# Backward states of an mLSTM moved up among the last key sweeps, and seven chunks instead of four taken ahead of the attention stage

## The chip, the cores and the metric

The kernel runs on one core of a Trainium2 chip. The metric is the device time of one execution in microseconds (us); lower is better. Engines are named as in the profile: PE is TensorE (matmuls), PEld its weight loads, DVE VectorE, ACT ScalarE, POOL GpSimd, and SP the engine whose queue issues most of the DMAs. Every engine works through its own instructions in program order.

## The reference

One bidirectional encoder layer on 2048 tokens of 1024 channels. What matters here is the mLSTM group (4 heads of 128 channels), a scan in each direction, and what surrounds it:

```python
u = _rms_norm(h, norm_mix_g[l]);  proj = u @ w_in[l]
hy = _short_conv_centred(proj[..., :HY_COLS], ...)          # Hyena: long convolutions
y_hy = _group_rms_norm(_hyena(hy, spec, hy_skip[l]), ...)
qk = silu(_short_conv_centred(proj[..., HY_COLS:off], ...)) # queries and keys of the mLSTM
y_ml = _mlstm_bidirectional(q, k, v, o_pre, gates, ml_gate_b[l])
h = h + concatenate([y_hy, _group_rms_norm(y_ml, ...)]) @ w_out[l]
h = h + _cross_attention(_rms_norm(h, ...), _rms_norm(mem, ...), wq, wk, wv, wo)
h = h + square(relu(_rms_norm(h, ...) @ ff_w1[l])) @ ff_w2[l]
return _rms_norm(h, final_norm_g)

# one chunk of the mLSTM, per head; C, n, m are the carried state
s   = einsum('td,sd->ts', qc, kc) * w
num = s @ vc + inter * (qc @ C);   den = sum(s) + inter * (qc @ n)
h   = num / max(|den|, exp(-m_t))
C   = carry_decay * C + einsum('s,sd,se->de', we, kc, vc)
```

The backward direction is the same scan on the flipped sequence; both directions are added.

## The kernel before

The kernel writes the work of many generators; each `yield` is a point at which another may go on. The program's main function (`program`, from line 2100) combines them with a few helpers: `chain` one after the other, `weave` two in proportion to costs, `among(g, h, n)` one step of `h` behind each n-th step of `g` and the rest of `h` at the end, `beside_each(g, h)` a step of `h` behind every step of `g`. A scheduler then fixes the order on each engine: it goes by the written order and by its own estimate of when inputs are ready, so that work of one generator can stand among another's where buffers and data allow. PSUM is two sets of four banks, `mm` and `hy`, handed out in turn; who takes a bank waits until its user of four turns before has been read.

The stages around the change, in order of time:

- **Key sweeps and natural products** (`sweep`, `natural`, lines 748 to 897). The input projection is done for half the tokens at a time. Columns are swept transposed (q, k and the Hyena inputs), each product as three matmuls (`mm3`, L355, L358, L359) with its operands split into a high and a low part. Columns 8 and 9 are the keys. Values and the output gate are done in natural order by `natural`; tiles 0 and 1 are the values. The second half of the tokens (rows 1024 and up) is done first, the first half last. The **Hyena** convolution (`hyena`, L956, L987, L1030, L173 and L186 on PE) is woven in.
- **Gates** (`gates`, lines 1076 to 1174): six steps, which turn the gate columns into decays and weights (`cols`). They stand behind every second step of the sweep of columns 4, 5, 8, 9 of the first half.
- **Backward states** (`states` and `backward`, lines 1209 to 1225): 15 updates from chunk 15 down to chunk 1, a chunk being 128 tokens. An update loads keys `kn` and values `va` (L1178, L1184, two buffers of each), scales the values on POOL (L1196), makes four products on PE (L1200, `hy<-va,kn`), adds them to the decayed state on DVE (L1206) and stores it with a POOL DMA (L1219, `cbd`). In the kernel before they begin behind the products of the values of the first half, one step behind each step of values, columns 6 and 7, and tile 2; what is left of them follows at the end.
- **Memory's products** (`memproj`, from line 693): 128 products L708, 64 keys' products L725 and 32 values' products L737 in plain float32, in which one instruction is two records of the trace. Their weights come by `wm` loads (L415).
- **Chunks of the mLSTM** (`mlstm`, lines 1227 to 1364): for each of 16 chunks the scores (L1284, made one chunk ahead), their masked exponentials (POOL L1290 and L1291, ACT L1293, DVE L1275 and L1294), 16 products with values and states (L1322 `hy<-va,rw` and L1324 `hy<-cf,rw` or `hy<-cbn,rw`; the very first chunk has no forward state and so 12), the division on ACT and DVE (L1327 to L1338), and the update of the forward state (L1200 `hy<-ve,kn`, then DVE L1202 or L1206 into `cf`). Chunk 0 needs the last backward state, which is loaded as `cbn` (L1258). Behind each odd chunk two chunks are normalised together on DVE (`bank_rsqrt`, L211 to L216, then L1356).
- **Attention stage** (`attention`, from line 1438): it transposes the mixed rows (L1479), splits them into `act`, multiplies them by `w_out`, and goes on to the cross-attention. Its first four token groups need chunks 0 to 3 of the mLSTM.

In the kernel before, `take(m, 5)` takes the set-up of the chunks and chunks 0 to 3 behind the steps of the memory's products; chunks 4 to 15 are then woven with the attention stage.

Of the kernel before, what the change touches and what calls it, by code (L numbers as in the profile page):

```python
# [2076 lines left out]
def chain(*gens):  # L2077
    for g in gens:
        yield from g


def weave(a, b, wa, wb, until=False):
    da = db = 0.0
    fa = fb = False
    while not (fa and fb):
        if fb or (not fa and da / wa <= db / wb):
            try:
                da += next(a)
            except StopIteration:
                fa = True  # L2090
        else:
            try:
                db += next(b)
            except StopIteration:
                fb = True
                if until:
                    return


def program(p):  # L2100
    with ExitStack() as ms:
        with ExitStack() as es:
            p.inproj_open(es)
            p.filters_open()
            p.prepq = p.x_first()
            p.pop()
            s = chain(p.sweep(range(4), 0, True, lambda: p.prep_x(1)), p.opened(), p.sweep(range(4), 1, False))
            f = p.filters()
            for _ in range(5):
                next(s)  # L2110
            next(f)
            next(f)
            next(s)
            weave(s, f, 140, 102, True)
            p.gates_open(es)
            n = p.memproj()
            m = p.mlstm(ms)
            with ExitStack() as hs:
                rest = chain(s, p.sweep(range(4, 10), 1, True), p.natural(1, (3, 0, 1, 2), True),
                             p.natural(0, (3,)), among(p.sweep((4, 5, 8, 9), 0, False), p.gates(), 2),  # L2120
                             among(chain(p.natural(0, (0, 1)), p.sweep((6, 7), 0, False),
                                         p.natural(0, (2,), p.prep_mem, 2)), p.states(), 1),
                             )
                weave(rest, p.hyena(hs), 445, 329)
            for _ in chain(p.turned_in(), take(n, 1), beside_each(n, take(m, 5))):
                pass
        with ExitStack() as rs:
            p.ts = rs.enter_context(ExitStack())
            p.tail_open(p.ts)
            with ExitStack() as at:  # L2130
                g = p.attention(at)
                weave(g, m, 440, 112, True)
                ms.close()
                p.ffn_open(rs)
                for _ in g:
                    pass
            p.ffn()


def among(g, h, every):  # L2140
    for i, v in enumerate(g):
        yield v
        if i % every == every - 1:
            next(h, None)
    for _ in h:
        pass


def beside_each(g, h):
    for v in g:  # L2150
        yield v
        yield next(h, 0)
    yield from h


def take(g, n):
    for _ in range(n):
        v = next(g, None)
        if v is None:
            return  # L2160
        yield v
# [31 lines left out]
```

## Time and profile before

| | |
|---|---|
| three timed runs | 3066.46, 3072.43, 3081.08 us (median 3072.43) |
| profiled execution's own time | 3076.22 us |
| its span | 3074.5 us |
| mean granted TensorE clock | 0.987 |
| last backward update on PE | 1086.33 us |
| DVE, ACT, POOL busy in the span | 63%, 49%, 41% |
| HBM traffic over the span | 196 GB/s |

Times within the trace are us from the start of the span. A row of the timeline gives the start, the length, engine, line, operation, what is written from what, the shape, and how many records were merged; in square brackets stands how long the engine had been idle before it and what ended the wait. A row of the windows gives the length of a stretch, then busy time and records of each engine, the granted TensorE clock (1.00 is full speed), the DMA engines' busy share and GB/s. Lengths of single matmuls overlap; how long one really takes is the distance of two starts.

### The profile page before, as it was taken

Reading aid. Unit: us, or ns where it says so; the run is one execution under the profiler, and the core shown is the slowest. Engines: PE = TensorE matmul, PEld = TensorE weight load, DVE = VectorE, ACT = ScalarE, POOL = GpSimd, SP = SyncE. Lnnn points to the kernel's source line nnn. Section 1 sums busy time; section 2 is a strip of 40 time slices with the busy share of each in tenths; the row PEclk is TensorE's granted clock in tenths of the full one; section 3 lists DMA queues with packets and bytes.
Section 4 is the critical chain, followed back from the end, with each engine's and each line's share of the span. In section 5 each row is a group of like instructions: output and inputs, shape, how many; then the busy total and the mean of one; then the engine's idle time right before and its main releaser. Section 6 shows DMA issues by size and latency. Waiting matters only on the chain.

```text
span 3074.5 us, 44129 instructions
## 1 busy us (share of the span) xinstructions
PE 2984.5 (97%) x14799; PEld 2369.8 (77%) x14799; DVE 1938.8 (63%) x3442; ACT 1493.0 (49%) x2930; POOL 1259.7 (41%) x1025
## 2 busy tenths in 40 slices
PE   9999999998999988999999999999999999999998
PEld 7666667775678757888887888888888888888876
DVE  7855454657656347867665665557555676566695
ACT  6443455635654236555544455556555543333335
POOL 0112123411344654333133247765566374344653
PEclk9999999999999988999999999999999999999999
DMA  6655687596877965464567466657544565344434
GB/s 219 196 188 171 214 271 219 184 297 200 258 223 249 349 231 192 158 220 131 188 203 259 147 210 216 208 181 243 186 154 151 195 198 171 118 158 120 155 103 164
DMA packets 423643, 607.03 MB, mean 197 GB/s; under 512 B 36846, under 2 KB 229998, under 8 KB 422392
## 3 DMA queue, kind: packets, MB, share of 16 engines
q1 hardware_dynamic: 395972, 525.42, 53.3%
q0 software_dynamic: 18992, 62.96, 5.6%
q10 hardware_dynamic: 8452, 15.83, 1.4%
q8 instruction: 117, 1.92, 0.3%
q14 instruction: 110, 0.90, 0.1%
HBM read 401.67 MB, written 202.41 MB: 196 GB/s over the span
## 4 chain that ended last, share of the span: by engine, by line
PE 58%; DVE 2%; DMA 1%; issue 1%; ACT 0%; POOL 0%; SPq 0%; DVEq 0%; ACTq 0%; POOLq 0%
PE mm L355 12%; PE mm L359 12%; PE mm L358 12%; PE hy L355 6%; PE hy L359 6%; PE hy L358 6%; PE hy L1322 1%; PE hy L1324 1%; DVE bl L1693 0%; PE hy L1284 0%; PE hy L1479 0%; PE hy L1596 0%; DVE acc L1991 0%; PE hy L1200 0%; DVE acc L2028 0%
## 5 line engine op out<-in xcount | busy, mean ns | idle before, releaser
L1692 ACT CAST ah<-w 128x512 fp32r<-128x512 f32 x284 | 176.7, 623 | 304.0 <-PE hy L358 157.8
L1693 DVE TENSOR_TENSOR bl<-wr,bh 128x512 fp32r<-128x512 f32 x213 | 235.5, 1110 | 131.1 <-ACT bh L1692 131.0
L366 DVE TENSOR_TENSOR wl<-wn,wh 128x512 fp32r<-128x512 f32 (+1 forms) x296 | 216.6, 775 | 94.3 <-ACT wh L366 94.3
L355 PE MATMUL mm<-xh,wh 128*128 128x512 f32 x640 | 263.3, 413 | 3.7 <-ACT wh L366 1.2
L358 PE MATMUL mm<-xl,wh 128*128 128x512 f32 x640 | 254.1, 397 | 4.5 <-DVE xl L366 4.4
L1692 ACT CAST bh<-wr 128x512 fp32r<-128x512 f32 x232 | 143.4, 621 | 229.0 <-PE mm L359 177.5
L359 PE MATMUL mm<-xh,wl 128*128 128x512 f32 x640 | 253.7, 397 | 0.0
L1693 DVE TENSOR_TENSOR al<-w,ah 128x512 fp32r<-128x512 f32 x236 | 213.6, 905 | 55.7 <-ACT ah L1692 55.6
L359 PE MATMUL mm<-bh,al 128*128 128x512 f32 x576 | 223.7, 391 | 4.0 <-DVE al L1693 4.0
L355 PE MATMUL mm<-bh,ah 128*128 128x512 f32 x576 | 225.8, 392 | 0.1
L358 PE MATMUL mm<-bl,ah 128*128 128x512 f32 x576 | 224.9, 390 | 0.0
L366 ACT CAST wh<-wn 128x512 fp32r<-128x512 f32 (+1 forms) x296 | 164.4, 620 | 105.8 <-PE mm L359 51.0
L358 PE MATMUL mm<-act,wh 128*128 128x512 f32 x512 | 202.0, 394 | 0.0
L355 PE MATMUL mm<-act,wh 128*128 128x512 f32 x512 | 199.4, 396 | 2.0 <-ACT wh L366 1.9
L359 PE MATMUL mm<-act,wl 128*128 128x512 f32 x512 | 199.9, 392 | 0.0
L355 PE MATMUL hy<-bh,ah 128*128 128x512 f32 x448 | 175.2, 391 | 0.0
L358 PE MATMUL hy<-bl,ah 128*128 128x512 f32 x448 | 174.6, 390 | 0.0
L359 PE MATMUL hy<-bh,al 128*128 128x512 f32 x448 | 174.4, 390 | 0.0
L331 POOL TENSOR_TENSOR b<-b 128x512 f32<-128x512 f32 x32 | 48.1, 1505 | 294.6 <-DVE b L330 275.2
L355 PEld LDWEIGHTS mm<-xh,wh 128*128 128x128 f32 x640 | 120.5, 188 | 53.1 <-issue 19.4
L358 PEld LDWEIGHTS mm<-xl,wh 128*128 128x128 f32 x640 | 120.6, 188 | 49.2 <-issue 18.6
L355 PE MATMUL mm<-wh,xh 128*128 128x256 f32 (+1 forms) x512 | 154.7, 302 | 0.0
(396 smaller groups left out, 8262.9 us busy)
## 6 DMA issues: line engine op xcount, KB each, us to landing
wr<-hc SPq DMA_DIRECT2D x224, 256.0 KB
w<-in_ff_w_dram SPq DMA_DIRECT2D x172, 256.0 KB
hc<-wn SPq DMA_DIRECT2D x128, 256.0 KB
wn<-in_w_in_dram SPq DMA_DIRECT2D x100, 256.0 KB
hc<-q SPq DMA_DIRECT2D x96, 256.0 KB
fs<-a SPq DMA_DIRECT2D x32, 512.0 KB
zs<-a POOLq DMA_DIRECT2D x32, 512.0 KB, 6.0
a<-fs SPq DMA_DIRECT2D x64, 256.0 KB
```

Source lines behind the costliest of these rows:

```text
L331: nc.gpsimd.tensor_tensor(b, f, b, ALU.subtract)
L355: first = mm(ps, lh, rh, start=start, stop=False)
L358: mm(ps, lh, rl, start=False, stop=False)
L359: self.last = mm(ps, ll, rh, start=False, stop=stop)
L366: both = (self.nc.scalar.copy(hi, src), self.nc.vector.tensor_tensor(lo, src, hi.bitcast(F32), ALU.subtract))
L1322: nc.tensor.matmul(dst, nm[:, h], va[:, h], start=True, stop=state is None)
L1324: nc.tensor.matmul(dst, rows_[d, 1][:, h], state[:, h], start=False, stop=True)
L1692: self.nc.scalar.copy(hi, src)
L1693: eng.tensor_tensor(lo, src, hi.bitcast(F32), ALU.subtract)
```

## The change

Three things are changed, all in `program`; one helper is new. First, the sweep of columns 4, 5, 8, 9 and the values' products are now one series of 20 steps, behind which a table, `(0, 1) * 6 + (2,) * 6 + (2, 0)`, places the steps of the gates (1) and of the backward states (2): the six gate steps stand where they stood, and seven steps of the states follow behind the last four steps of the sweep and the first three of the values. Second, the rest of the states stands behind the steps of columns 6 and 7 and tile 2. Third, `take(m, 8)` takes chunks 0 to 6 of the mLSTM ahead of the attention stage instead of chunks 0 to 3. No computation is added or removed.

```diff
                 rest = chain(s, p.sweep(range(4, 10), 1, True), p.natural(1, (3, 0, 1, 2), True),
-                             p.natural(0, (3,)), among(p.sweep((4, 5, 8, 9), 0, False), p.gates(), 2),
-                             among(chain(p.natural(0, (0, 1)), p.sweep((6, 7), 0, False),
-                                         p.natural(0, (2,), p.prep_mem, 2)), p.states(), 1),
+                             p.natural(0, (3,)),
+                             paced(chain(p.sweep((4, 5, 8, 9), 0, False), p.natural(0, (0, 1))),
+                                   p.gates(), back := p.states(), (0, 1) * 6 + (2,) * 6 + (2, 0)),
+                             among(chain(p.sweep((6, 7), 0, False), p.natural(0, (2,), p.prep_mem, 2)), back, 1),
                              )
                 weave(rest, p.hyena(hs), 445, 329)
-            for _ in chain(p.turned_in(), take(n, 1), beside_each(n, take(m, 5))):
+            for _ in chain(p.turned_in(), take(n, 1), beside_each(n, take(m, 8))):
                 pass
...
+def paced(g, h1, h2, plan):
+    for v, n in zip(g, plan):
+        yield v
+        if n:
+            next((h1, h2)[n - 1], None)
+    yield from g
```

What this does to the order of instructions shows at three places. First PE at the end of the memory's products, where L708 and L737 are the memory's products, L1284 the scores of chunks 0 and 1, and L1322 and L1324 the products of chunk 0. Before:

```order
L186 MATMUL hy<-a,e_2743 32x512 x7
L708 MATMUL mm<-mt,wm 128x256 x10
L737 MATMUL mm<-wm,kt 128x512 x10
L1284 MATMUL hy<-qn,kk_t 128x128 x8
L737 MATMUL mm<-wm,kt 128x512 x6
L1322 MATMUL hy<-va,rw 128x129 x5
L1324 MATMUL hy<-cbn,rw 128x129
```

In the changed kernel PE has at this place:

```order
L708 MATMUL mm<-mt,wm 128x256 x7
L1284 MATMUL hy<-qn,kk_t 128x128 x8
L708 MATMUL mm<-mt,wm 128x256 x9
L737 MATMUL mm<-wm,kt 128x512
L1322 MATMUL hy<-va,rw 128x129 x5
L1324 MATMUL hy<-cbn,rw 128x129
```

The scores stand nine products L708 and ten L737 earlier, and one product of the values, not six, stands between them and chunk 0. The 15 that are left stand among the rows of chunks 0 and 1: seven behind chunk 0, two and one around the scores of chunk 2, two among chunk 1's first products, and three ahead of its update.

The second place is DVE between the first chunk and the first split of the attention stage's operand (`act`). Each `cf` is the forward state behind a chunk (the first of its two rows is shown), the number only telling one tile from another. Before:

```order
L1202 COPY cf_10062<-hy_10068 128x258
L1206 SCALAR_TENSOR_TENSOR cf_10219<-cf_10062,cols_9877,hy_10225 128x129 x2
L1206 SCALAR_TENSOR_TENSOR cf_10404<-cf_10219,cols_9877,hy_10410 128x129 x2
L1206 SCALAR_TENSOR_TENSOR cf_10555<-cf_10404,cols_9877,hy_10561 128x129 x2
L366 TENSOR_TENSOR act_10775<-hy_10776,act_10774 128x4x128
```

In the changed kernel DVE has ahead of that split:

```order
L1202 COPY cf_10062<-hy_10068 128x258
L1206 SCALAR_TENSOR_TENSOR cf_10219<-cf_10062,cols_9877,hy_10225 128x129 x2
L1206 SCALAR_TENSOR_TENSOR cf_10404<-cf_10219,cols_9877,hy_10410 128x129 x2
L1206 SCALAR_TENSOR_TENSOR cf_10555<-cf_10404,cols_9877,hy_10561 128x129 x2
L1206 SCALAR_TENSOR_TENSOR cf_10732<-cf_10555,cols_9877,hy_10738 128x129 x2
L1206 SCALAR_TENSOR_TENSOR cf_10877<-cf_10732,cols_9877,hy_10883 128x129 x2
L1206 SCALAR_TENSOR_TENSOR cf_11029<-cf_10877,cols_9877,hy_11035 128x129 x2
L366 TENSOR_TENSOR act_11107<-hy_11108,act_11106 128x4x128
```

Seven chunks instead of four are updated before the attention stage's operand is split, and no row of the memory's products or of the attention stage's products stands among chunks 2 to 6 on PE. Behind chunks 1, 3 and 5 the normalisation of two chunks stands on DVE ahead of the next chunk's division, as it does behind chunk 1 in the kernel before. Four splits of the attention stage's first weights (L366, `wl`), which before stand between the second and the third of these rows, now stand ahead of the first.

The third place is SP's queue in the key sweeps, in one piece of the difference; `kn<-kn` and `va<-vd` are the loads of a backward update, `kn<-st` stores of the key sweep, `a<-fs` and `dm` loads of the Hyena convolution:

```order
 L944 DMA dm<-in_c_dm_dram 128x256
 L920 DMA a<-fs_391 128x1x512
-L849 DMA kn<-st 128x4x128 x2
+L849 DMA kn<-st 128x4x128
+L1178 DMA kn<-kn 128x512
+L1184 DMA va<-vd 128x4x128
+L849 DMA kn<-st 128x4x128
 L858 DMA kn<-st 16x128
```

The third update's loads move up into the sweep's stores, and those of the later ones move up in the same way; on PE 11 updates instead of 8 are done when columns 6 and 7 have been swept. The first two pairs of loads stand, but for one row, where they stood.

## Prediction

> **What bounds the kernel now.** The page says how full PE is over the whole span, and the table of windows says where it is not. From the page, the line of busy times:
>
> ```profile
> PE 2984.5 (97%) x14799; PEld 2369.8 (77%) x14799; DVE 1938.8 (63%) x3442; ACT 1493.0 (49%) x2930; POOL 1259.7 (41%) x1025
> ```
>
> PE is idle for 3074.5 - 2984.5 = 90 us. A change of order can gain only there, or where the granted clock is under 1.00. The windows around the change (columns: stretch, length, busy time and records of PE, PEld, DVE, ACT, POOL, then clock, DMA share, GB/s):
>
> ```profile
> 985.00:1115.00 130.00, 124.75 (x607) 93.67 (x607) 52.58 (x164) 32.60 (x72) 78.28 (x94) 0.97 0.93 313
> 1137.00:1157.00 20.00, 11.06 (x50) 9.75 (x49) 15.46 (x55) 9.25 (x38) 8.43 (x8) 0.59 0.43 135
> 1157.00:1179.00 22.00, 15.45 (x87) 14.48 (x88) 14.71 (x50) 14.44 (x54) 9.13 (x8) 0.73 0.51 157
> 1179.00:1295.00 116.00, 115.91 (x634) 100.02 (x633) 91.52 (x246) 62.35 (x193) 44.20 (x37) 1.00 0.54 175
> 1295.00:1310.00 15.00, 9.75 (x44) 7.62 (x43) 12.84 (x33) 12.97 (x43) 2.37 (x2) 0.77 0.54 169
> 1310.00:1510.00 200.00, 199.50 (x1090) 171.11 (x1089) 141.23 (x357) 108.94 (x317) 58.22 (x47) 1.00 0.50 160
> 1122.00:1179.00 57.00, 36.19 (x208) 0.74 0.59 190
> ```
>
> The last row is PE alone. Three regimes follow one another. The memory's products keep PE 96% busy at 0.97. Then comes a hole: from 1122 to 1179 PE is busy for 36.19 of 57 us, and at 0.74; that is 36.19 x 0.74 = 26.8 us of work at full clock, so 30 us are lost. From 1179 on, in the attention stage, PE is full but for one gap near 1300. The PE timeline tells what is in the hole (start, length, ..., idle before):
>
> ```profile
> 1036.71 1.06 PE L1200 MATMUL hy<-va,kn 128*128 128x129 f32 x8
> ...
> 1086.33 1.16 PE L1200 MATMUL hy<-va,kn 128*128 128x129 f32 x8 [2.94 <-POOL va L1196]
> ...
> 1102.05 4.58 PE L708 MATMUL mm<-mt,wm 128*128 128x256 f32 x20
> 1106.47 8.75 PE L737 MATMUL mm<-wm,kt 128*128 128x512 f32 x20
> 1115.05 1.95 PE L1284 MATMUL hy<-qn,kk_t 128*128 128x128 f32 x16
> 1116.84 5.32 PE L737 MATMUL mm<-wm,kt 128*128 128x512 f32 x12
> 1121.99 1.28 PE L1322 MATMUL hy<-va,rw 128*128 128x129 f32 x10
> ...
> 1125.57 1.23 PE L1200 MATMUL hy<-ve,kn 128*128 128x129 f32 x8 [0.74 <-ACT ht L1336]
> 1126.80 1.16 PE L1284 MATMUL hy<-qn,kk_t 128*128 128x128 f32 x8
> 1127.80 0.39 PE L1322 MATMUL hy<-va,rw 128*128 128x129 f32 x2
> ...
> 1135.22 0.67 PE L1322 MATMUL hy<-va,rw 128*128 128x129 f32 x2 [4.58 <-DVE den L1330]
> ...
> 1136.97 1.92 PE L1200 MATMUL hy<-ve,kn 128*128 128x129 f32 x8
> ...
> 1149.84 0.77 PE L1322 MATMUL hy<-va,rw 128*128 128x129 f32 x2 [2.81 <-DVE bry L213]
> ...
> 1156.92 2.09 PE L1200 MATMUL hy<-ve,kn 128*128 128x129 f32 x8 [2.12 <-ACT ht L1336]
> ...
> 1165.63 1.23 PE L1200 MATMUL hy<-ve,kn 128*128 128x129 f32 x8 [0.36 <-ACT ht L1336]
> ...
> 1174.90 1.12 PE L1479 MATMUL hy<-ident,wn 128*128 128x128 f32 x4 [5.17 <-DVE act L366]
> ...
> 1179.10 1.49 PE L355 MATMUL mm<-act,wh 128*128 128x512 f32 x4
> ...
> 1190.90 1.05 PE L1200 MATMUL hy<-ve,kn 128*128 128x129 f32 x8
> ```
>
> The four chunks that are meant to lie beside the memory's products lie behind them: chunk 0 starts at 1121.99, when the last of those products ends, and the four updates of the forward state (`ve,kn`) start at 1125.57, 1136.97, 1156.92 and 1165.63. The first attention product is at 1179.10. In between PE follows a chain through ACT, DVE and POOL, 11.4, 20.0 and 8.7 us from one update to the next. The 20.0 is explained by DVE's timeline, where the normalisation behind an odd chunk first waits for its sums and then holds up the next chunk:
>
> ```profile
> 1142.54 1.13 DVE L1338 SCALAR_TENSOR_TENSOR ht<-hy,den,ht 128x128 f32<-128x128 f32 x4
> 1146.68 0.17 DVE L211 TENSOR_SCALAR hy<-brm 128x8 int32<-128x8 int32 x1 [3.02 <-ACT brm L208]
> ...
> 1150.43 2.22 DVE L1356 SCALAR_TENSOR_TENSOR ht<-ht,hy,gml 128x128 f32<-128x128 f32 x8
> ...
> 1153.83 0.14 DVE L1330 TENSOR_TENSOR den<-hy,cols 128x4 f32<-128x4 f32 x1
> ```
>
> Chunk 1 is divided by 1143.7, but the next division (L1330) comes at 1153.83, 10 us later. A chunk without a normalisation took 8.7 us.
>
> **The change part by part.** *The states, earlier.* Three of the 15 updates leave the stretch of the memory's products for the key sweeps. An update is 1.06 us of PE wherever it stands:
>
> ```profile
> 843.59 1.06 PE L1200 MATMUL hy<-va,kn 128*128 128x129 f32 x8
> ```
>
> PE is as full in the one place as in the other, so the 3 x 1.06 us only move. The last update now stands where the twelfth stood, at 1036.71, 50 us ahead of the old last one at 1086.33, and the 2.94 us wait there goes. SP could load the last state as `cbn` only at 1093:
>
> ```profile
> 1093.11 0.80 SPq L1258 DMA_DIRECT2D cbn<-cbd  x2
> ```
>
> That load now stands ahead of the last twelve weight loads and of two Hyena steps' loads on SP, which queue behind it if the state is late; 50 us earlier it should not be. Each moved update also takes its loads past SP's loads for the Hyena convolution, its scaling past POOL's multiplications and its store past POOL's stores; who waits for those is PE's Hyena products. Over all 15 updates PE waited for `va` once (in all, times, longest):
>
> ```profile
> PE hy L1200 <- POOL va L1196: 2.9, 1, 2.9
> ```
>
> I take nothing for the new places, bounds 0 and +4 us (one more such wait, and its clock).
>
> *The end of the memory's products.* By the rows above, 20 records of L708 take 1106.47 - 1102.05 = 4.42 us and 20 of L737 8.58 us, and an instruction is two records. The scores of chunk 0 come nine L708 (4.0 us) and ten L737 (8.6 us) earlier, and the 15 L737 left behind chunk 0 are 12.9 us of cover for chunks 0 and 1. That cover is all that lies beside chunks. PE's work up to chunk 1's update is the old end of the products less the wait, 1121.99 - 2.94 = 1119.05, and 12 products of chunk 0 (2.7 us), its update (1.05), the scores of chunk 2 (1.0) and 16 products of chunk 1. A product (two records) takes 0.224 us: eleven start from 1127.80 on before the row at 1130.26 below, so 16 are 3.6 us.
>
> ```profile
> 1130.26 0.39 PE L1324 MATMUL hy<-cbn,rw 128*128 128x129 f32 x2
> ```
>
> The sum is 1119.05 + 8.35 = 1127.4. The four splits of the attention's first weights move in here; on DVE they took 3.2 us:
>
> ```profile
> L366 DVE TENSOR_TENSOR wl<-we,wh 128x512 fp32r<-128x512 f32 x4 | 3.2, 842 | 0.0
> ```
>
> I add half of that: chunk 1's update at 1129 instead of 1136.97, 8 us gained (bounds 1126, PE alone without the splits and at a better clock, and 1133, with the old 4.58 us wait on top).
>
> *The bare chunks.* Chunks 2 to 6 have nothing beside them. From chunk 1's update to chunk 6's are three intervals behind an odd chunk and two behind an even one. An odd one is 20.0 us less the splits that have left it, of which I take 2.5: 17.5. The sum is 3 x 17.5 + 2 x 8.7 = 69.9 us, with ends at 77.4 (no gain from the splits) and 43.5 (8.7 each). Chunk 6's update starts at 1129 + 69.9 = 1198.9.
>
> *The start of the attention.* From chunk 3's update to the first attention product it was 1179.10 - 1165.63 = 13.5 us, with 5.17 us behind the normalisation of chunks 2 and 3. Chunk 6 is even and has none behind it: 8.3 us (ends 8.3 and 13.5). The first attention product comes at 1207.2, 28.1 us later than before.
>
> *The attention, relieved.* Chunks 4 to 6 no longer lie among its products. PE was full there, so what goes is PE time: 3.6 us of products, 1.05 of update (the row at 1190.90) and 1.0 of scores, 5.65 a chunk, 17.0 in all. The gap near 1300 lost 15 - 9.75 x 0.77 = 7.5 us; it lies where the softmax's transposes wait, among others, for chunks' DVE work, and chunks of other numbers will lie there, so I count none of it (end: -7.5).
>
> The sum: +28.1 - 17.0 = **+11.1 us**. A second reckoning, cruder: 30 us were lost on four bare chunks, 7.5 each; five bare ones lose 7.5 more. From 3076.2 of the profiled execution (span 3074.5 and 1.7 around it) the sum gives 3087.3; that execution is 3.8 above the median of the runs shown, so on their scale I forecast 3072.4 + 11 = **3083 us**.
>
> *The clock.* In the stretch 1295 to 1310 the granted clock fell to 0.77 with no wait of PE longer than this one:
>
> ```profile
> 1301.18 0.66 PE L1479 MATMUL hy<-ident,wn 128*128 128x128 f32 x4 [1.75 <-DVE act L366]
> ```
>
> So I let the bare chunks run at the clock that is in their measured intervals. If the clock stayed at 1.00 from chunk 2 on, PE's excess in the hole, 36.19 - 26.8 = 9.4 us or 2.35 a chunk, would be saved on five bare chunks, 11.8 us, and the sum would be -0.7. The Trainium skill (TensorE: Matmul & The Clock Gate, "HAM oscillation — how this bites in real kernels") puts the limit at idle gaps of more than about 3.4 us; by that rule this is how it would go, for the 4.58 us wait gets cover and the 2.81 us one would not count. The row above speaks against the rule.
>
> **The rivals.** *Slower by more than the sum: the normalisation stays as long as it was.* The place is DVE behind chunks 1, 3 and 5. If the splits were not on the chain of the 20.0 us, each odd interval stays at 20.0 (+7.5 in all), and if the attention's start meets chunk 6's own waits it stays at 13.5 (+5.2): +23.8, 3096 us. It decides from 18.9 us per odd interval on, where the sum passes +15.4. For it speaks that ACT and POOL have part in that chain, against it that the splits stood directly ahead of a division. *Faster: the chunks flow.* If seven chunks in a row settle at the 8.7 us of the undisturbed one, the five cost 43.5 and the sum is 11.1 - 26.4 = -15.3, 3057 us. Against it speaks that DVE's order has the normalisation ahead of the next division each time. *No change: the attention gives back more.* If the gap near 1300 goes with the chunks (-7.5), the sum is +3.6, 3076 us. *No change: the clock stays up*, -0.7, 3072 us, as worked out above; for it speaks that the longest wait behind 1137 was 2.81 us, against it the 0.77. *It doesn't do what it says*: that is partly so by the order already, since the chunks stand behind the products as before; it is in the forecast.
>
> **How the numbers follow.** About 0.5%, 15.4 us, is what a measurement of this kernel can tell from no change. The forecast's case has 0.58, with a range of its own from 3070 (update at 1126, odd intervals at 15, relief of 20) to 3092 (update at 1133, odd ones at 19); 0.16 of it lies over 3088. The slower rival has 0.18, the faster 0.09, the attention's 0.08, the clock's 0.07; of the last two 0.03 passes -15.4 together with chunks that flow. Faster 0.09 + 0.03 = 0.12, same 0.42 + 0.12 = 0.54, slower 0.16 + 0.18 = 0.34. The range from 3063 to 3100 leaves out the faster rival's end and the worst of the slower one.
>
> **What would show it.** Right: chunk 1's update 6 to 10 us earlier than 1137, three odd intervals of 16 to 19 us, the first attention product between 1198 and 1214, no wait for `va` beyond 1050, and a full PE from there on. Wrong: odd intervals near 9 (faster rival) or 20 (slower rival); PE waits for `va`, `zs` or `zg` between 780 and 900, or `cbn` holding SP before the last weights; or a gap near 1300 that is gone or doubled.

## The result and the profile after

The changed kernel takes 3081.67 us (median of 20 runs, 3076.27 to 3094.67), the kernel before 3073.85 us in the same comparison (20 runs). The ratio is 1.0025, 95% interval 1.0017 to 1.0032: 7.7 us slower, which is real and less than 0.5%. The profiled execution took 3077.49 us (span 3075.8), 1.3 us more than that of before. The two are not typical: this one lies 4.2 us below the median of its kernel, that of before 2.4 above its own, and 1.3 + 4.2 + 2.4 is, but for rounding, the 7.8 us between the medians. So the traces are read below for places and intervals, and the runs for sums.

The page's line of busy times:

```profile
PE 2982.7 (97%) x14799; PEld 2368.6 (77%) x14799; DVE 1944.2 (63%) x3442; ACT 1493.2 (49%) x2930; POOL 1263.1 (41%) x1025
```

The windows (stretch, length, busy time and records of PE, PEld, DVE, ACT, POOL, then granted clock, DMA share, GB/s). The first stretch is that of the memory's products, the last is the bare chunks as a whole:

```profile
985.00:1115.00 130.00, 128.23 (x677) 99.74 (x676) 57.78 (x170) 36.95 (x89) 82.44 (x96) 1.00 0.95 328
1132.00:1137.00 5.00, 0.00 (x0) 0.02 (x1) 2.83 (x13) 1.79 (x11) 0.18 (x1) 0.77 0.79 242
1137.00:1148.00 11.00, 8.05 (x34) 7.47 (x35) 8.02 (x33) 5.58 (x23) 7.31 (x7) 0.50 0.33 117
1162.00:1172.00 10.00, 7.04 (x29) 6.48 (x30) 8.04 (x32) 4.56 (x17) 7.19 (x7) 0.50 0.29 105
1295.00:1310.00 15.00, 15.00 (x92) 13.28 (x91) 12.50 (x35) 8.96 (x34) 6.69 (x6) 1.00 0.60 190
1130.00:1200.00 70.00, 43.37 (x255) 40.34 (x254) 48.10 (x180) 36.69 (x158) 36.39 (x33) 0.73 0.49 158
```

PE is now full up to 1115 (128.23 of 130 us, before 124.75). The hole has become longer: 43.37 us of work in 70 us, at a clock of 0.73. The gap at 1295 is gone from its place; it stands at 1322 now, as one wait of 2.90 us, where PE waited four times between 1295 and 1304 before, 5.3 us in all. The PE timeline shows the hole chunk by chunk (start, length, ..., idle before):

```profile
1113.88 1.06 PE L1200 MATMUL hy<-ve,kn 128*128 128x129 f32 x8
...
1126.11 1.05 PE L1200 MATMUL hy<-ve,kn 128*128 128x129 f32 x8
...
1137.01 0.77 PE L1322 MATMUL hy<-va,rw 128*128 128x129 f32 x2 [5.11 <-DVE bry L213]
...
1144.09 2.09 PE L1200 MATMUL hy<-ve,kn 128*128 128x129 f32 x8 [2.12 <-ACT ht L1336]
...
1152.10 1.23 PE L1200 MATMUL hy<-ve,kn 128*128 128x129 f32 x8 [0.37 <-ACT ht L1336]
...
1169.11 2.09 PE L1200 MATMUL hy<-ve,kn 128*128 128x129 f32 x8 [2.12 <-ACT ht L1336]
...
1176.56 1.23 PE L1200 MATMUL hy<-ve,kn 128*128 128x129 f32 x8 [0.36 <-ACT ht L1336]
...
1194.16 2.09 PE L1200 MATMUL hy<-ve,kn 128*128 128x129 f32 x8 [0.97 <-ACT ht L1336]
...
1201.47 1.19 PE L355 MATMUL mm<-act,wh 128*128 128x512 f32 x4
```

Chunk 1's update stands at 1126.11, chunk 6's at 1194.16. In between the intervals behind odd chunks are 18.0, 17.0 and 17.6 us, behind even ones 8.0 and 7.5. The first attention product follows at 1201.47, 22.4 us later than before. What PE waits for from 1125 to 1200 (in all, times, longest):

```profile
PE hy L1322 <- DVE bry L213: 15.3, 3, 5.2
PE hy L1200 <- ACT ht L1336: 5.9, 5, 2.1
```

The three waits of 5 us are the normalisations behind chunks 1, 3 and 5. On DVE one of them looks like this:

```profile
1128.28 1.12 DVE L1338 SCALAR_TENSOR_TENSOR ht<-hy,den,ht 128x128 f32<-128x128 f32 x4
...
1133.86 0.17 DVE L211 TENSOR_SCALAR hy<-brm 128x8 int32<-128x8 int32 x1 [3.94 <-ACT brm L208]
...
1135.58 1.28 DVE L1294 TENSOR_TENSOR rw<-rw,hy 128x512 f32<-128x512 f32 x2
...
1137.60 2.22 DVE L1356 SCALAR_TENSOR_TENSOR ht<-ht,hy,gml 128x128 f32<-128x128 f32 x8
...
1140.99 0.15 DVE L1330 TENSOR_TENSOR den<-hy,cols 128x4 f32<-128x4 f32 x1
```

DVE stands 3.94 us in front of the normalisation, waiting for sums that come through POOL and ACT, and behind it in DVE's order are the product of scores and decay that chunk 2's next products need (1135.58) and chunk 2's division (1140.99). PE waits for DVE, and DVE for something that nobody needs yet.

The relief in the attention stage is read at two of its products that stand in both kernels (L1656). In the kernel before:

```profile
1374.11 1.02 PE L1656 MATMUL hy<-ssum,ones 128*128 128x512 f32 x2
1541.45 1.02 PE L1656 MATMUL hy<-ssum,ones 128*128 128x512 f32 x2
```

In the changed kernel:

```profile
1393.96 1.02 PE L1656 MATMUL hy<-ssum,ones 128*128 128x512 f32 x2
1544.06 1.02 PE L1656 MATMUL hy<-ssum,ones 128*128 128x512 f32 x2
```

Of the 22.4 us, 19.9 are left at the first and 2.6 at the second. They come back late: the chunks take turns with the attention's products as before, and the relief falls due when the chunks run out earlier (their last product, L1322, starts at 1433.5 instead of 1502.8).

### The profile page after: what moved, and what is told of

It reads as the page before. It is cut to its first block, busy times and chain, and to the rows that moved or that the text cites. A ratio compares the mean times of both kernels' runs of the same rounds, so it can differ in the third digit from the quotient of the medians.

```text
span 3075.8 us, 44181 instructions
## 1 busy us (share of the span) xinstructions
PE 2982.7 (97%) x14799; PEld 2368.6 (77%) x14799; DVE 1944.2 (63%) x3442; ACT 1493.2 (49%) x2930; POOL 1263.1 (41%) x1025
## 4 chain that ended last, share of the span: by engine, by line
PE 56%; DVE 3%; DMA 2%; ACT 1%; issue 1%; POOL 0%; SPq 0%; DVEq 0%; ACTq 0%; POOLq 0%
PE mm L355 12%; PE mm L359 12%; PE mm L358 12%; PE hy L359 6%; PE hy L355 6%; PE hy L358 6%; PE hy L1322 1%; PE hy L1324 1%; DVE bl L1693 1%; PE hy L1200 0%; PE hy L1479 0%; DVE acc L1991 0%; PE hy L1284 0%; DMA wr<-xs 0%; PE hy L1596 0%
## 5 line engine op out<-in xcount | busy, mean ns | idle before, releaser
L366 DVE TENSOR_TENSOR wl<-wn,wh 128x512 fp32r<-128x512 f32 (+1 forms) x296 | 212.9, 764 | 95.4 <-ACT wh L366 95.4
L366 ACT CAST wh<-wn 128x512 fp32r<-128x512 f32 (+1 forms) x296 | 164.7, 620 | 121.5 <-PE mm L358 49.6
L1522 POOL TENSOR_TENSOR ssum<-ssum,sq 128x512 f32<-128x512 f32 x56 | 80.7, 1440 | 197.7 <-ACT sq L1521 188.7
```

The source lines that it names most:

```text
L366: both = (self.nc.scalar.copy(hi, src), self.nc.vector.tensor_tensor(lo, src, hi.bitcast(F32), ALU.subtract))
L1522: nc.gpsimd.tensor_tensor(ssum, ssum, sq, ALU.add)
```

## The experiments

All were timed against the kernel before (median 3071.8 to 3072.6 us beside them); ratios are to it. The comparison with the changed kernel goes by its 1.0025 (1.0017 to 1.0032).

**1 and 2: each half alone.** The early states with four chunks (of the changed kernel):

```diff
-            for _ in chain(p.turned_in(), take(n, 1), beside_each(n, take(m, 8))):
+            for _ in chain(p.turned_in(), take(n, 1), beside_each(n, take(m, 5))):
```

> Only the first half of the change: the backward states among the gates and the last key sweeps, and four chunks written beside the memory's products as before. My theory (the states' move gains a little at the end of the products, the three more bare chunks cost more than that): chunk 3's update near 1152 as in the changed kernel (before: 1165.6), the first attention product near 1166 instead of 1179.1, the attention itself as long as before, so 8 to 13 us faster than before, ratio 0.9957 to 0.9974. Rival A (what the change costs comes from the moved states, by more work and waits in the key sweeps): as slow as the changed kernel, ratio about 1.0025. Rival B (a faster head is swallowed again in the attention, whose chunks' DVE work sets its pace): ratio within 0.001 of 1.

Measured: 3061.5 us, ratio 0.9968 (0.9956 to 0.9980), 9.8 us faster than before. Its PE timeline:

```profile
1130.27 1.05 PE L1200 MATMUL hy<-ve,kn 128*128 128x129 f32 x8
...
1148.86 2.09 PE L1200 MATMUL hy<-ve,kn 128*128 128x129 f32 x8 [2.13 <-ACT ht L1336]
...
1157.26 1.23 PE L1200 MATMUL hy<-ve,kn 128*128 128x129 f32 x8 [0.37 <-ACT ht L1336]
...
1170.58 1.35 PE L355 MATMUL mm<-act,wh 128*128 128x512 f32 x4
```

Seven chunks with the late states is the same edit on the kernel before, 5 become 8:

```diff
-            for _ in chain(p.turned_in(), take(n, 1), beside_each(n, take(m, 5))):
+            for _ in chain(p.turned_in(), take(n, 1), beside_each(n, take(m, 8))):
```

> Only the second half: seven chunks written ahead of the attention, the backward states where they were. My theory: each of the three more chunks costs what a bare one takes (20.0 and 8.7 us in turn) less the 5.65 us of TensorE time that it saves in the attention; chunk 6's update near 1165.6 + 20.0 + 8.7 + 20.0 = 1214, less about 4 for the weight splits that move, the first attention product near 1220, 41 later than before, relief 17 to 20: 20 to 24 us slower than before, ratio 1.0065 to 1.008. Rival A (the states are what costs): within 0.001 of 1. Rival B (chunks outside the attention are free, since the attention is relieved by as much): within 0.002 of 1.

Measured: 3093.92 us, ratio 1.0073 (1.0060 to 1.0086), 22.4 us slower. Its PE timeline:

```profile
1136.90 1.93 PE L1200 MATMUL hy<-ve,kn 128*128 128x129 f32 x8
...
1156.87 2.09 PE L1200 MATMUL hy<-ve,kn 128*128 128x129 f32 x8 [2.13 <-ACT ht L1336]
...
1215.53 1.18 PE L355 MATMUL mm<-act,wh 128*128 128x512 f32 x4
```

What follows: the change is a gain of about 10 us and a loss of over 20 in one. In run 1 the first attention product comes 8.5 us earlier than before, in run 2 it comes 36 us later. The moved states cost nothing that the comparison can see, and the second half is what makes the kernel slower; both rivals of both runs fall. The interval behind chunk 1 is 20.0 us in run 2, where the weight splits stand in it. Where they don't it is 18.0 (the changed kernel) and 18.6 (run 1), and run 2's other two odd intervals are 17.0 and 17.4.

**3: four output buffers instead of two** (on the changed kernel, to see whether the next chunk waits for the stores):

```diff
-                    y = sb.tile([128, 4, 128], F32, tag="h0", name="ht", bufs=2)
+                    y = sb.tile([128, 4, 128], F32, tag="h0", name="ht", bufs=4)
```

> The changed kernel with four buffers for a chunk's output (ht) instead of two, nothing else. Theory N (the odd chunks' 17 to 18 us are the normalisation that VectorE and TensorE wait for): only the store's part of the wait goes (chunk 1's outputs landed at 1141.6 and 1142.6, its buffer is written again from 1143.4 on), so intervals behind odd chunks stay at 16 to 18 us and the time within 3 us of the changed kernel, 3079 to 3083. Theory S (the next chunk waits until the outputs are stored and the buffers are free): intervals behind odd chunks fall to 9 to 12 us, 15 to 24 us faster than the changed kernel, about 3060. The order of the head may move a little with the memory's layout: the first scores stand 12 products earlier.

Measured: 3072.36 us, ratio 1.0001 (0.9990 to 1.0013), so 0.24% or 7 us faster than the changed kernel; between the two expectations. The rows of its PE timeline:

```profile
1121.99 1.05 PE L1200 MATMUL hy<-ve,kn 128*128 128x129 f32 x8
1132.71 0.61 PE L1200 MATMUL hy<-ve,kn 128*128 128x129 f32 x4
...
1143.09 1.23 PE L1200 MATMUL hy<-ve,kn 128*128 128x129 f32 x8 [0.98 <-ACT ht L1336]
...
1152.60 0.77 PE L1322 MATMUL hy<-va,rw 128*128 128x129 f32 x2 [3.00 <-DVE bry L213]
...
1159.68 2.09 PE L1200 MATMUL hy<-ve,kn 128*128 128x129 f32 x8 [2.12 <-ACT ht L1336]
...
1192.77 1.18 PE L355 MATMUL mm<-act,wh 128*128 128x512 f32 x4
```

Behind chunk 3 the interval is still 16.6 us with its wait for the normalisation, and behind chunk 5 it is 17.1: the buffers are not what the chain waits for. Behind chunk 1 it fell to 10.7. There the order that the scheduler makes has changed: the start of chunk 2's division (L1330, L1331) now stands ahead of chunk 1's eight L1356. The head moved too: chunk 1's update is at 1122.0 instead of 1126.1, which is about half of the 8.7 us that the first attention product gains. Why more buffers move the head wasn't traced.

**4: the normalisation written later** (on run 3; behind chunks 1, 3 and 5 it is called after the next chunk's update):

```diff
-            if n % 2:
-                rv = self.bank_rsqrt(sb, ss, 128)
...
+            if n in (1, 3, 5):
+                late.append(partial(normalise, self, sb, gml, ym, stores, n, ss, ys))
+            elif n % 2:
+                normalise(self, sb, gml, ym, stores, n, ss, ys)
+            if late and n % 2 == 0:
+                late.pop()()
+                while n % 4 == 0 and stores:
+                    stores.pop()()
```

> The run with four output buffers, and the normalisation behind chunks 1, 3 and 5 written behind the next chunk's update instead of ahead of its scores' product and division. Theory N (the normalisation on VectorE holds the chain): intervals behind chunks 1, 3 and 5 fall from 17 to 18 us to 9 to 12, three times 6 to 8 us: 18 to 24 us faster than the run with four buffers alone, 3055 to 3062. Theory C (the chunk's own chain through ScalarE, VectorE and GpSimd takes that long, the normalisation lies beside it): less than 6 us faster than that run.

Measured: 3066.58 us, ratio 0.9984 (0.9975 to 0.9994), 5.8 us faster than run 3 where 18 to 24 were expected. Its PE timeline:

```profile
1125.88 1.06 PE L1200 MATMUL hy<-ve,kn 128*128 128x129 f32 x8
...
1147.66 1.93 PE L1200 MATMUL hy<-ve,kn 128*128 128x129 f32 x8
...
1156.48 1.23 PE L1200 MATMUL hy<-ve,kn 128*128 128x129 f32 x8 [0.96 <-ACT ht L1336]
...
1175.69 1.23 PE L1200 MATMUL hy<-ve,kn 128*128 128x129 f32 x8 [0.97 <-ACT ht L1336]
...
1185.52 1.17 PE L355 MATMUL mm<-act,wh 128*128 128x512 f32 x4
```

The intervals behind chunks 3 and 5 fell from 16.6 and 17.1 to 8.8 and 8.7 us, so the place of the cost is shown: the normalisation in DVE's order. The size was wrong, and by the time alone theory C (less than 6 us) would have held: the intervals decide, not the time. Chunk 1's interval had already gone to 10.7 in run 3 and only came to 9.3, and the normalisation now lengthens the even intervals (10.4 to 12.4, 8.8 to 10.5). The five intervals take 49.8 us instead of 63.5, which is 13.7 less. Of these, 3.9 are lost ahead of them (chunk 1's update comes at 1125.9 instead of 1122.0) and 2.6 behind them (from chunk 6's update to the first attention product it is 9.8 us instead of 7.2). So 7.3 us are left at the first attention product, near the 5.8 of the runs. Why the head came later again wasn't traced.

**5: the waits filled** (on the changed kernel; nine products that nothing reads, between the forward and the backward products of chunks 2, 4 and 6):

```diff
+                if d == 0 and n in (2, 4, 6):
+                    for _ in range(9):
+                        nc.tensor.matmul(pn[:, 264:512], nm[:, 0], qn.rearrange("p h t -> p (h t)")[:, 0:248], start=True, stop=True)
```

> The changed kernel with nine products of 128x248 that nothing reads, put between the forward and the backward products of chunks 2, 4 and 6, where TensorE waited 5.0 to 5.2 us for VectorE. Each is about 0.42 us at full clock, nine 3.8 us. Theory K (the granted clock falls because TensorE idles, and the slow clock lengthens the chunks): the clock in the bare stretch rises from about 0.75 to 0.9 or more, the chunks' own products shorten by about 2 us each, and the time falls by 4 to 10 us against the changed kernel, to 3072 to 3078. Theory D (the chain through VectorE, ScalarE and GpSimd sets the pace, TensorE's clock hardly): the clock rises or not, the intervals behind odd chunks stay within 1 us of 17.0 to 18.0, and the time is within 4 us of the changed kernel, or above it where the fill is longer than the wait.

Measured: 3074.4 us, ratio 1.0009 (1.0000 to 1.0018), 0.16% or 5 us faster than the changed kernel (7 by the medians), with more work; the two intervals only just touch. The same window as the last of the changed kernel's above, then two rows of the PE timeline:

```profile
1130.00:1200.00 70.00, 54.72 (x341) 49.70 (x342) 52.51 (x194) 41.43 (x168) 38.57 (x36) 0.88 0.59 188
```

```profile
1159.11 3.93 PE L1328 MATMUL hy<-qn,rw 128*128 128x248 f32 x18
...
1167.24 1.23 PE L1200 MATMUL hy<-ve,kn 128*128 128x129 f32 x8 [1.24 <-ACT ht L1339]
```

The clock rises from 0.73 to 0.88, and the intervals behind odd chunks are 16.2, 13.5 and 13.5 us instead of 18.0, 17.0 and 17.6; the even ones become 9.2 instead of 8.0 and 7.5. From chunk 1's update to chunk 6's PE is busy for 34.9 us with other work than the fill, instead of 39.6: that is 4.7 of the 6.4 us by which the five intervals shrink, 0.9 a chunk where theory K had said 2. So theory K holds in the clock and in the time, at about half its size per chunk. It is not quite alone: in DVE's order the division and the forward state's update (L1206) have changed places in chunks 2 to 4, which may have part in the shorter odd and the longer even intervals; that wasn't separated. By this reading a wait of 5 us costs twice: once itself, and again in the half-speed products of the 10 us behind it.

**6 and 7: Hyena sooner.** Why do the chunks not lie beside the memory's products, though the last backward update starts at 1040? PSUM banks are handed out in the order in which the program is written, and the first chunk is written behind the whole Hyena branch. In the changed kernel the last read of a Hyena bank, on DVE, and the first scores, on PE, stand close together:

```profile
1096.07 1.22 DVE L1064 TENSOR_TENSOR a<-a,hy 128x1024 f32<-128x1024 f32 x1
...
1098.67 1.95 PE L1284 MATMUL hy<-qn,kk_t 128*128 128x128 f32 x16
```

The scores start 1.4 us behind the end of that read and 58 us behind the last backward update. In run 1 the read ends at 1101.44 and the scores start at 1102.82, in the kernel before the two are 1115.68 and 1115.05. So the early states moved the chunks' start about as far as Hyena's end moved with them, by 16 us against 18, and not to where the states end. (The rows show this order in time; they do not name the bank.) Hyena's steps were then dealt out sooner (on run 1; run 7 also has four output buffers):

```diff
-                weave(rest, p.hyena(hs), 445, 329)
+                weave(rest, p.hyena(hs), 445, 380)
```

> The early states with four chunks (the first experiment) and the Hyena branch's steps dealt out sooner among the key sweeps: the weight 329 in the weave becomes 380. Theory H (what keeps the chunks behind the memory's products is Hyena's end: the PSUM banks are handed out in the order of the program, so the first scores wait for Hyena's last bank near 1100, not for the states): the first scores stand 81 of the memory's 224 products ahead of their end instead of 25, the four updates 58, 38, 16 and 3 ahead, and TensorE loses 12 to 20 us less between 1100 and the first attention product: 3042 to 3052, ratio 0.990 to 0.9935. Rival (the chunks compete with the memory's products and Hyena for VectorE, ScalarE and GpSimd, so the stretch stays as long; or the sweeps wait for Hyena's denser loads): 3058 to 3070, as the first experiment or slower.

> The same with four output buffers. The first scores stand 66 products ahead of the end, the updates 48, 34, 18 and 3. Theory H: as the run before within 4 us, 3042 to 3054; the buffers no longer matter, since the chunks stand beside other work. If the buffers alone made the gain of the third experiment (9 us against the changed kernel), this run is 6 to 9 us faster than the one without them.

Measured: 3060.34 us, ratio 0.9962 (0.9950 to 0.9975), and 3062.8 us, 0.9969 (0.9959 to 0.9980): no different from run 1. Both expectations of a gain fell, the mechanism didn't. Two windows of run 6:

```profile
440.00:700.00 260.00, 239.09 (x1513) 176.13 (x1512) 140.31 (x227) 131.62 (x237) 74.17 (x91) 0.98 0.77 247
985.00:1155.00 170.00, 169.08 (x953) 140.79 (x952) 75.62 (x240) 70.27 (x194) 95.17 (x109) 1.00 0.84 282
```

The first of these in run 1:

```profile
440.00:700.00 260.00, 253.07 (x1527) 190.09 (x1526) 148.76 (x242) 142.45 (x255) 81.66 (x93) 0.99 0.75 238
```

In run 6 PE is full until 1155 with all four chunks inside. The last Hyena bank is read by 1044.35, and the first scores (1085.49) now follow the last backward update (1084.60). The first attention product comes 10.4 us behind the last of the memory's products instead of 40.7, but this counts the cover too high (so does the 30 us in the expectation of run 9 below), for those products end 25 us later than in run 1: the attention begins only 5.0 us earlier (1165.57 instead of 1170.58). PE idles 13.0 us less than in run 1 between 985 and 1230, and 12.6 us more before 985, with 14.0 us of PE time lost from 440 to 700. The longest waits of PE from 300 to 1000 in run 6, 19.5 us in all, are for Hyena's loads, for which run 1 waits 6.2 us:

```profile
PE hy L1030 <- DMA a<-zs: 8.0, 1, 8.0
PE hy L173 <- DMA a<-zg: 5.8, 4, 2.2
PE mm L956 <- DMA a<-fs: 5.7, 3, 4.7
```

So the cover of the chunks can be bought, at the price that it is worth. The output buffers give nothing here, as expected.

**8 to 10: what is best.** Run 1 with four output buffers and the normalisation of chunks 0 and 1 behind chunk 2's update (`n in (1,)` in the edit of run 4), Hyena as before; then the same with Hyena's weight at 345 and at 341.

> Early states, four chunks, four output buffers, the normalisation of chunks 0 and 1 written behind chunk 2's update; Hyena as it was. If the gains of the first experiment (10.3 us against before) and of the buffers (9.3 us against the changed kernel, from the earlier head) add up, and the late normalisation gives 2 to 4 us on its single odd interval: 3049 to 3054. If the buffers' gain belongs to the seven bare chunks alone: 3058 to 3062.

> Early states, four chunks, four output buffers, late normalisation of chunks 0 and 1, and Hyena's steps only a little sooner (329 becomes 345). The first scores stand 56 of the memory's products ahead of their end instead of 37, the updates 40, 23, 9 and 0. Theory H with the price seen at 380 (there the cover of the chunks gained 30 us and the key sweeps lost as much to waits for Hyena's loads, 14 us of them before 700): a third of the shift costs a third, about 5 to 9 us, and three of four chunks get cover, 10 to 20 us: 3040 to 3050. Rival (a shift pays for itself and no more): 3051 to 3057.

> The same with 341. Scores 51 products ahead, the updates 34, 11, 0 and 0. Theory H: two of four chunks get cover, 6 to 14 us less, and 4 to 7 us are lost in the sweeps: 3043 to 3052. Rival: 3051 to 3057.

Measured: 3053.52 us, ratio 0.9937 (0.9925 to 0.9950); 3063.01, 0.9972 (0.9961 to 0.9984); 3053.82, 0.9941 (0.9923 to 0.9958). Run 8 is 8 us below run 1 (9.5 by the ratios), as it should be if the gain of run 3 and the 2 to 4 us expected of the late normalisation add to it; these two were not separated here. It beats both kernels, the one before by 0.63%. Theory H fell again as a way to gain time: 341 is the same as run 8, and 345 is slower, outside both of its expectations. PE idles 11 us more than in run 8 before 985 there, and 2.4 us less from 985 to 1230.

## Why the prediction held, step by step

The range (3063 to 3100) and the sign hold, and the ratio is within 0.5% as most likely. That the time is only 1.3 us from the one predicted is partly luck: the change was forecast as 11.1 us and measured as 7.7, and the kernel before came out 1.4 us slower in this comparison than the median on which the forecast stands. Most of the signs came out as named: the odd intervals, the first attention product at 1201.5, no wait for `va`. Two did not: chunk 1's update came 10.9 us earlier and not 6 to 10, and the gap near 1300 did not stay but moved and shrank. The terms:

- **The states, earlier** (0, bounds 0 and +4): right. No wait for `va` is left, and run 1 shows no cost.
- **The end of the products** (8 us gained): too small. Chunk 1's update came at 1126.1, 10.9 us earlier and at the favourable bound of 1126 that was PE's own work without the wait and the splits; the clock from 985 to 1115 was 1.00 instead of 0.97. The first scores came 16.4 us earlier (1098.67 instead of 1115.05).
- **The bare chunks** (69.9 us): 68.0. The odd intervals of 17.0 to 18.0 hit the 17.5, the even ones of 7.5 and 8.0 are a little under 8.7. That the splits were in the 20.0 is shown by run 2: the intervals without them are 1.4 to 3.0 us shorter, where 2.5 had been taken. That the rest is the normalisation is shown by run 4.
- **The attention's start** (8.3 us): 7.3.
- **The relief** (-17.0): 19.8 by the rows at 1541 and 1544, and part of the gap near 1300 went as well, the 7.5 us that was named and not counted (waits of 5.3 us became one of 2.90).

All of these errors go the same way, 8.5 us in all. The traces sum to +22.4 - 19.8 = +2.6 us, and the runs say +7.7. The two traced executions lie 6.6 us closer together than the medians of their kernels, and where in the kernel that much goes between executions wasn't traced, so the terms are checked by single executions and the sum by the runs. The crude second reckoning, 7.5 us for one more bare chunk, was the nearer one, partly by chance. The two halves alone add up to +12.6, 4.9 more than both together; the intervals of the three comparisons leave about 6 us for such a difference, so it is not shown to be one.

Of the rivals, the slower one falls with the odd intervals, the faster one with the normalisation that stayed in DVE's order; run 4 shows that its 8.7 us are what an odd interval takes without it, while all five take 49.8 us and not its 43.5. The rival of an attention that gives back more came true in part, since the gap near 1300 shrank: the traces' +2.6 is nearer to its +3.6 than to the forecast's sum. The rival of the clock was rightly set aside for the kernel as it is: the clock did not stay up. But the reason given, short waits, was not put to the test, because the waits behind odd chunks came out at 5.0 to 5.2 us, longer than the 2.81 us that the rival reckoned with. Run 5 gives its size: 6.4 us less on the five bare intervals (61.6 instead of 68.0) for a clock of 0.88, where 11.8 had been worked out for 1.00.

What the prediction did not see is why so little lies beside the memory's products: Hyena's banks stand ahead of the chunks'. The rows of L1064 and L1284 and run 6 show it, and runs 6, 7 and 9 that it could not be had for nothing.

## What to carry to other kernels

Work that is written beside a busy stage lies beside it only if every resource it takes comes free early enough, and a pool that hands out buffers in program order can be the one that doesn't; look in the order of the built program, not in the source. Split a change that does two things into its halves before judging it: here one was worth 10 us and hidden by the other. In a bare chain, ask which step in an in-order queue nobody is waiting for, and put it behind the step that somebody is.

## What the runs showed of the chip

The granted clock falls to 0.50 in a wait of 5 us and stays there for 10 us or more behind it (the rows 1137 to 1148 and 1162 to 1172 above), with two more waits of 0.8 and 2.1 us on the way. A shorter one is enough: in run 3 the wait of 3.00 us at 1152.60 is followed by this window:

```profile
1152.60:1156.00 3.40, 2.59 (x10) 2.29 (x11) 3.30 (x15) 0.00 (x0) 0.64 (x2) 0.50 0.00 0
```

The Trainium skill (TensorE: Matmul & The Clock Gate, "HAM oscillation — how this bites in real kernels") names gaps of more than about 3.4 us. The 5 us waits agree with that; the 3.00 us one, and the 1.75 us one of the prediction (with waits of 1.38 and 1.63 us on either side of it, at a clock of 0.77), are under it.

The length of the longest wait alone does not decide. In the kernel before, a wait of 1.82 us that ends at 148.73 is followed by 0.50 from 148.89 to 152.30; in the changed kernel the same wait (1.82 us, ending at 148.54) is not, nor is one of 2.63 us that ends at 644.29. Counted over the traces of both kernels and the ten runs, for waits that begin at full clock: of those from 2.65 us up 72 of 73 came with a stretch of 0.50 in them or within 3.4 us behind them, of those from 2 to 2.65 us 20 of 36, of those from 1.3 to 2 us 36 of 103. In all these traces the clock is either 0.50 or 1.00, and the stretches of 0.50 behind waits last whole multiples of 3.41 us (in the changed kernel 13.65 us from 1134.66 on and 10.24 us from 1161.96 on).

So for planning the limit should be taken nearer to 2 us in this kernel, and several short waits close together count as well. The other surprise is that useless products in such a wait made a kernel faster.
